# Two blocks of a weight tile begin 32 bytes further at the entries of the gate and up passes

## The chip, the cores and the metric

The kernel runs on one core of one Trainium2 chip. The metric is the device time of one execution in microseconds; of several runs the median is given. A profiled execution is a run of its own: its span reaches from the first to the last instruction, and its time is a little longer.

## The reference

The reference is a small decoder trunk in float32: 256 tokens of width 1024, two layers. Each layer has an attention (16 heads of 64; the first layer with forget gates, the second with a relative-position bias, both causal), a SwiGLU feed-forward part and a gated embedding, and a last RMSNorm ends the trunk. The change lies in the feed-forward part:

```python
u = _rmsnorm(h, ffn_norm_g[i])
gu = u @ ffn_w_in[i]                       # (256, 1024) @ (1024, 2 * 2816)
h = h + (jax.nn.silu(gu[..., :D_FF]) * gu[..., D_FF:]) @ ffn_w_out[i]
```

## The kernel before

All weights are packed into one array of 216 tiles, in the order in which they are used, each of 128 partitions x 1024 float32. `half` (line 110) brings in the next tile: SP starts its DMA into `raw` (six buffers), ScalarE rounds it to float32r as `hi` (line 122), and VectorE writes the remainder `raw - hi` as `lo` (line 123). `hi` and `lo` have six buffers each, in tiles of 1024 + 64 columns.

Every product of two float32 operands a and b is made of three matmuls in `mm3` (lines 76 to 80), all into the same accumulator: hi of a with hi of b (line 78), hi of a with lo of b (line 79), lo of a with hi of b (line 80). a is the operand that stays in the array, its weights; b streams through. So of three matmuls two load weights from the hi of a and the third from its lo.

There are two ways to use a tile of the packed array. In the q and k projections and in the gate and up passes the tile holds eight blocks of 128 columns, one for each 128 rows of the contraction, and a block is the weights; the normalised activations g (128 x 256 for each block) stream. `blocks` (line 126) makes these. In the other products (v, wo, the second feed-forward product fo, pu, pg) the weights are activations, and the tile streams in pieces of 512 columns, in the last gate partly of 256.

Where the operands lie: all tiles named here begin at a multiple of 256 bytes, which the kernel calls a line (`LINE = 64` float32). `blocks` asks `half` for a start 16 columns further (`APART = 16`), that is 64 bytes past the line; a block is 512 bytes long, so all its eight blocks begin 64 bytes past a line. g, and tiles that stream, begin on a line.

The feed-forward part (`ffn`) works in pieces f of 128 of the 2816 hidden columns, 22 in all. For each f there are two tiles, gate (a = 0) and up (a = 1), each of 8 blocks x 3 = 24 matmuls into bank gu. `up([0, 1])` is written apart, since the norm's second half is made in its midst. Behind it the order of TensorE's work is, in each layer:

- f = 2: the gate tile, then the four matmuls of `nm.spread` (pr, line 175), then the up tile
- f = 3: gate and up
- down for f = 0 and 1: 24 matmuls of 512 columns into the four banks fo
- f = 4, 5: gate, up, gate, up, without a break: 96 matmuls; then down for f = 2 and 3
- and so on to f = 20, 21, behind which the last down products, the embedding's product pu and the residual follow.

All work of an engine is issued in program order. A tile's DMA and its two passes on ScalarE and VectorE are issued as far ahead as the six buffers let them.

Names that the profile uses: gu is the accumulator of gate and up, whi and wlo are the hi and lo tiles, fh and fl the hi and lo of the gated product, pq the accumulator of the q and k projections, sp the attention scores, L78 to L80 the three matmuls of `mm3`.

Of the kernel before, what the change touches and what calls it, by code (L numbers as in the profile page):

```python
# [28 lines left out]
F32R = mybir.dt.float32r  # L29
AF = mybir.ActivationFunctionType  # L30
ALU = mybir.AluOpType

P = 128
S = 256
D = 1024
KT = D // P
# [10 lines left out]
HW = 1024  # L47
# [7 lines left out]
LINE = 64  # L55
APART = 16


@with_exitstack
def trunk(ctx: ExitStack, tc: tile.TileContext, x, xt, pt, w, wf, cst, gains, gf, bf, rel, hot, rvm, out):  # L60
    nc = tc.nc
    one = ctx.enter_context(tc.tile_pool(name="one", bufs=1))
    work = ctx.enter_context(tc.tile_pool(name="work", bufs=2))
# [4 lines left out]
    def bank(name):  # L68
        return ps.tile([P, 512], F32, tag="bank", name=name)

    def f32(ap):
        return ap.bitcast(F32)
# [3 lines left out]
    def mm3(o, a, b, start, stop):  # L76
        (ah, al), (bh, bl) = a, b
        mm(o, ah, bh, start=start, stop=False, skip_group_check=True)  # L78
        mm(o, ah, bl, start=False, stop=False, skip_group_check=True)  # L79
        mm(o, al, bh, start=False, stop=stop, skip_group_check=True)  # L80
# [26 lines left out]

    state = {"next": 0}

    def half(at=0):  # L110

        i = state["next"]
        state["next"] += 1
        raw = work.tile([P, HW], F32, tag="raw", bufs=RAW, name=f"raw{i}")
        hi, lo = (work.tile([P, HW + LINE], F32R, tag=n, bufs=6, name=f"{n}{i}")[:, at:at + HW] for n in ("whi", "wlo"))
        parts = 2 if i < 2 else 1
        for q in range(parts):
            c = slice(q * HW // parts, (q + 1) * HW // parts)
            if i == 0 and q == 1:
                nc.sync.dma_start(hx[:, 1], xt[:, 1])  # L120
            nc.sync.dma_start(raw[:, c], w[i][:, c])
            nc.scalar.activation(hi[:, c], raw[:, c], AF.Copy)  # L122
            nc.vector.tensor_tensor(lo[:, c], raw[:, c], f32(hi[:, c]), op=ALU.subtract)  # L123
        return hi, lo

    def blocks():

        return [t.rearrange("p (k c) -> p k c", k=KT) for t in half(APART)]


    class Norm:
# [51 lines left out]

    nm = Norm(0)
    first = [half()]
    nm.block(0, hx[:, 0])
    nm.block(1, hx[:, 1])
    first.append(half())
    for b in range(1, 4):
        nc.sync.dma_start(hx[:, 2 * b:2 * b + 2], xt[:, 2 * b:2 * b + 2])  # L190
# [29 lines left out]
    def split(hi, lo, src):  # L220
        nc.scalar.activation(hi, src, AF.Copy)  # L221
        nc.vector.tensor_tensor(lo, src, f32(hi), op=ALU.subtract)

    def tokens(o, x, t, w, start, stop):

        at = slice(t * P, (t + 1) * P)
        mm3(o, (x[0][:, at], x[1][:, at]), w, start, stop)
# [10 lines left out]
    def residual(hf, bks):  # L238
        for t in range(2):
            at = h[:, t, hf * HC:(hf + 1) * HC]  # L240
            nc.vector.tensor_tensor(at, at, bks[t], op=ALU.add)
# [67 lines left out]
    def attention(layer, nm, mid, early, nf):  # L309
        vb = [bank(f"v{layer}_{b}") for b in range(4)]  # L310
        rest = None
        for c in range(4):
            wt = [early.pop(0) if early else half() for _ in range(2)]
            for kk in range(2):
                hi, lo = wt[kk]
                k = 2 * c + kk
# [23 lines left out]
        for t in range(2):  # L340
            for hf in range(2):
                col = nm.col[:, t:t + 1]
                src = vb[2 * t + hf].rearrange("p (j s d) -> p j s d", s=2, d=DH)
                for s in range(2):
                    at = (slice(None), slice(4 * hf, 4 * hf + 4), slice(2 * s * DH, (2 * s + 1) * DH))
# [13 lines left out]
        def project(j, a):  # L359
            hi, lo = blocks()  # L360
            if a == 0:
                pq[j] = bank(f"pq{layer}_{j}")
            bk = pq[j]
            for k in range(KT):
                mm3(bk[:, a * S:(a + 1) * S], (hi[:, k], lo[:, k]), nm.k(k),
                    start=(k == 0), stop=(k == KT - 1))
            if a == 0:
                return
            del pq[j]
            t = work.tile([P, 2, S], F32, tag="qkt", name=f"qkt{layer}_{j}")  # L370
            nc.vector.tensor_tensor(t.rearrange("p a s -> p (a s)"), bk,
                                    nm.row.rearrange("p a s -> p (a s)"), op=ALU.mult)
            th = work.tile([P, 2, S], F32R, tag="qkh", name=f"qkh{layer}_{j}")
            tl = work.tile([P, 2, S], F32R, tag="qkl", name=f"qkl{layer}_{j}")
            split(th, tl, t)
            qk[j] = t, th, tl
# [54 lines left out]
        for j in range(NP):  # L431
            project(j, 0)
            if j >= 1:
                scores(j - 1)
            if j >= 2:
                transposes(j - 2)
            project(j, 1)
            if j >= 2:
                values(j - 2)
            if layer == 0 and j >= 4:  # L440
                moba[0](j - 4)
# [23 lines left out]
    def ffn(layer, nm, filler, np_):  # L465
        acc = []
        prod = {}

        def up(fs):

            bks = {f: bank(f"gu{layer}_{f}") for f in fs}

            def step(f, a, wt, k, start):
                mm3(bks[f][:, a * S:(a + 1) * S], (wt[0][:, k], wt[1][:, k]), nm.k(k), start, k == KT - 1)

            if fs[0] == 0:
                wts = {f: (blocks(), blocks()) for f in fs}
                for k in range(KT):
                    if k == 3:
                        nm.turn(1)  # L480
                        nm.square(1)
                    for f in fs:
                        for a in range(2):
                            step(f, a, wts[f][a], k, k == 0 and a == 0)
                nm.root()
                return fs, bks
            for a in range(2):
                wt = blocks()
                for k in range(KT):
                    step(fs[0], a, wt, k, k == 0)  # L490
                if fs[0] == 2 and a == 0:
                    nm.spread()
                    gated(*early)
            gated(fs, bks)

        def gated(fs, bks):
            for f in fs:
                t = work.tile([P, 2, S], F32, tag="t2k", bufs=3, name=f"gut{layer}_{f}")
                nc.vector.tensor_tensor(t.rearrange("p a s -> p (a s)"), bks[f],  # L499
                                        nm.row.rearrange("p a s -> p (a s)"), op=ALU.mult)  # L500
                sg = work.tile([P, S], F32, tag="sg", name=f"sg{layer}_{f}")
                nc.scalar.activation(sg, t[:, 0], AF.Silu)
                nc.vector.tensor_tensor(sg, sg, t[:, 1], op=ALU.mult)  # L503
                th = work.tile([P, S], F32R, tag="th", bufs=4, name=f"fh{layer}_{f}")
                tl = work.tile([P, S], F32R, tag="tl", bufs=4, name=f"fl{layer}_{f}")
                split(th, tl, sg)
                prod[f] = th, tl

        def down(f, wt):
            hi, lo = wt  # L510
            for t in range(2):
                for hf in range(2):
                    cols = slice(hf * HC, (hf + 1) * HC)
                    tokens(acc[hf][t], prod[f], t, (hi[:, cols], lo[:, cols]), f == 0, False)

        def last(f, hf):

            wt = half()
            for i in range(2):
                for t in range(2):  # L520
                    tokens(acc[hf][t], prod[f + i], t, [w[:, i * HC:(i + 1) * HC] for w in wt],
                           False, f + i == FT - 1)

        early = up([0, 1])
        acc.extend([bank(f"fo{layer}_{hf}_{t}") for t in range(2)] for hf in range(2))
        for f in range(2, FT, 2):
            up([f])
            up([f + 1])
            if f == FT - 6:
                pp = filler()  # L530
            if f < FT - 2:
                down(f - 2, half())
                down(f - 1, half())
        last(FT - 4, 0)
        filler(pp)
        last(FT - 2, 0)
        residual(0, acc[0])
        last(FT - 4, 1)
        np_.turn(0)
        np_.square(0)  # L540
        last(FT - 2, 1)
        residual(1, acc[1])
# [106 lines left out]
    for layer in range(2):  # L649
# [8 lines left out]
        nm = Norm(3) if layer == 0 else None  # L658
# [95 lines left out]
```

## Time and profile before

| what | value |
|---|---|
| time, median of 3 runs | 683.77 us (682.6 to 684.1) |
| the profiled execution's time | 684.86 us |
| its span | 683.1 us |
| TensorE busy with matmuls | 669.7 us, 98% of the span |
| TensorE loading weights | 614.9 us |
| VectorE busy | 453.3 us |
| ScalarE busy | 385.6 us |
| gu matmuls | 3 x 704 |

A matmul in a timeline has the start in microseconds, then how long it took. It is pipelined: the next one starts long before it is over, so what the stream costs is the distance from start to start, here called the pitch. The stretches that the profile can be asked for have the length, then for each engine the busy time with the count of instructions in brackets, and then the granted clock of TensorE (1.00 is full speed), the share of the DMA engines and the bytes moved in GB/s.

### The profile page before, as it was taken

To read this page: it belongs to the slowest core of one execution; us is meant where nothing else is said; L and a number is where in the kernel's file an instruction comes from. 1 tells how busy PE (TensorE), PEld (TensorE's weight loads), DVE (VectorE), ACT (ScalarE), POOL (GpSimd) and SP (SyncE) were. 2 spreads that over 40 slices of the span, in tenths; PEclk is the share of its full clock that TensorE was granted. 3 is DMA by queue.
4 is the path that set the end of the run, shared out by engine and by line. 5 is a ranking of instruction groups with operands and counts; after the bars stand their busy time and mean duration, and the time that the engine had idled before them with its cause. 6 is when DMAs were issued, how large, how long until landed. Compare 5 with 4: busy or idle time off the path is not lost.

```text
span 683.1 us, 11825 instructions
## 1 busy us (share of the span) xinstructions
PE 669.7 (98%) x4604; PEld 614.9 (90%) x4604; DVE 453.3 (66%) x782; ACT 385.6 (56%) x698; POOL 29.8 (4%) x57
## 2 busy tenths in 40 slices
PE   8998999999999999999999999999999999999994
PEld 6898998999999999998889999889999999999884
DVE  4688886666666666666676888765766666666673
ACT  6875665655444444447665766655544444444663
POOL 1057000000000000000000000000000000000000
PEclk9999999999999999999999999999999999999998
DMA  8979333455555555655576533343755555565401
GB/s 272 380 279 350 126 125 124 154 184 187 187 190 188 191 190 195 202 185 186 176 275 201 180 124 126 119 159 123 243 190 187 185 186 187 190 202 195 168 1 62
DMA packets 37529, 125.90 MB, mean 184 GB/s; under 512 B 4240, under 2 KB 7008, under 8 KB 37472
## 3 DMA queue, kind: packets, MB, share of 16 engines
q1 hardware_dynamic: 36016, 121.35, 52.5%
q0 software_dynamic: 608, 2.11, 1.0%
q10 hardware_dynamic: 848, 1.68, 0.7%
q8 instruction: 36, 0.59, 0.4%
q14 instruction: 21, 0.17, 0.1%
HBM read 124.03 MB, written 4.24 MB: 188 GB/s over the span
## 4 chain that ended last, share of the span: by engine, by line
PE 90%; DVE 0%; ACT 0%; issue 0%; POOLq 0%; DVEq 0%; POOL 0%; ACTq 0%
PE gu L80 12%; PE gu L79 12%; PE gu L78 12%; PE fo L78 6%; PE fo L79 6%; PE fo L80 6%; PE pq L78 4%; PE pq L80 4%; PE pq L79 4%; PE wo L78 2%; PE wo L80 2%; PE wo L79 2%; PE pg L78 2%; PE pg L80 2%; PE pg L79 2%; PE pp L413 2%
## 5 line engine op out<-in xcount | busy, mean ns | idle before, releaser
L123 DVE TENSOR_TENSOR wlo<-raw,whi 128x1024 fp32r<-128x1024 f32 (+1 forms) x218 | 264.9, 1218 | 162.6 <-ACT whi L122 162.4
L122 ACT ACTIVATE whi<-raw 128x1024 fp32r<-128x1024 f32 (+1 forms) x218 | 227.7, 1048 | 196.0 <-PE gu L79 75.0
L78 PE MATMUL gu<-g,whi 128*128 128x256 f32 x704 | 198.5, 282 | 0.0
L80 PE MATMUL gu<-g,wlo 128*128 128x256 f32 x704 | 198.2, 282 | 0.0
L79 PE MATMUL gu<-g,whi 128*128 128x256 f32 x704 | 198.1, 281 | 0.0
L79 PEld LDWEIGHTS gu<-g,whi 128*128 128x128 f32 x704 | 134.8, 191 | 0.7
L78 PEld LDWEIGHTS gu<-g,whi 128*128 128x128 f32 x704 | 132.4, 188 | 0.8
L80 PEld LDWEIGHTS gu<-g,wlo 128*128 128x128 f32 x704 | 132.4, 188 | 0.0
L78 PE MATMUL pq<-g,whi 128*128 128x256 f32 x256 | 74.7, 292 | 0.0
L80 PE MATMUL pq<-g,wlo 128*128 128x256 f32 x256 | 72.4, 283 | 0.0
L79 PE MATMUL pq<-g,whi 128*128 128x256 f32 x256 | 72.3, 283 | 0.0
L78 PE MATMUL fo<-whi,fh 128*128 128x512 f32 x176 | 69.0, 392 | 0.0
L79 PE MATMUL fo<-wlo,fh 128*128 128x512 f32 x176 | 68.8, 391 | 0.0
L80 PE MATMUL fo<-whi,fl 128*128 128x512 f32 x176 | 68.5, 389 | 0.0
L78 PEld LDWEIGHTS pq<-g,whi 128*128 128x128 f32 x256 | 48.9, 191 | 0.9 <-ACT vhi L347 0.6
L79 PEld LDWEIGHTS pq<-g,whi 128*128 128x128 f32 x256 | 49.3, 193 | 0.0
L80 PEld LDWEIGHTS pq<-g,wlo 128*128 128x128 f32 x256 | 49.0, 191 | 0.0
L221 ACT ACTIVATE fh<-sg 128x256 fp32r<-128x256 f32 x44 | 18.1, 415 | 47.6 <-DVE sg L503 47.6
L499 DVE TENSOR_TENSOR gut<-gu,row 128x512 f32<-128x512 f32 x44 | 30.0, 691 | 18.0 <-PE gu L80 18.0
L80 PEld LDWEIGHTS fo<-whi,fl 128*128 128x128 f32 x176 | 33.1, 188 | 7.0
L78 PEld LDWEIGHTS fo<-whi,fh 128*128 128x128 f32 x176 | 33.0, 188 | 6.3
L79 PEld LDWEIGHTS fo<-wlo,fh 128*128 128x128 f32 x176 | 33.1, 188 | 6.0
(137 smaller groups left out, 935.5 us busy)
## 6 DMA issues: line engine op xcount, KB each, us to landing
raw<-w SPq DMA_DIRECT2D x214, 512.0 KB, 3.3
d<-d SPq DMA_DIRECT2D x4, 768.0 KB, 12.5
bias<-cd POOLq DMA_DIRECT2D x4, 512.0 KB, 9.2
bias<-d SPq DMA_DIRECT2D x4, 512.0 KB, 5.1
raw<-w SPq DMA_DIRECT2D x4, 256.0 KB, 5.4
h<-x ACTq DMA_DIRECT2D x2, 512.0 KB, 5.3
hx<-xt SPq DMA_DIRECT2D x3, 256.0 KB, 5.3
p<-pt SPq DMA_DIRECT2D x2, 256.0 KB, 4.2
```

The source lines that it names most:

```text
L78: mm(o, ah, bh, start=start, stop=False, skip_group_check=True)
L79: mm(o, ah, bl, start=False, stop=False, skip_group_check=True)
L80: mm(o, al, bh, start=False, stop=stop, skip_group_check=True)
L122: nc.scalar.activation(hi[:, c], raw[:, c], AF.Copy)
L123: nc.vector.tensor_tensor(lo[:, c], raw[:, c], f32(hi[:, c]), op=ALU.subtract)
L221: nc.scalar.activation(hi, src, AF.Copy)
L413: nc.tensor.transpose(pp[:, q * P:(q + 1) * P], e[:, q * P:(q + 1) * P], ident)
L499: nc.vector.tensor_tensor(t.rearrange("p a s -> p (a s)"), bks[f], nm.row.rearrange("p a s -> p (a s)"), op=ALU.mult)
```

## The change

In some tiles the first two blocks of lo begin 32 bytes further than the others: `FURTHER = 8` columns are added to the 16 of `APART`, so they begin 96 bytes past the line. The other six begin one line behind their former place, so again 64 bytes past a line. `hi` stays as it was. To make room the lo tiles are one line wider, all of them. VectorE writes such a lo in two instructions, one for the two first blocks and one for the six others, where it wrote one.

These tiles are, in each layer, the up tile of f = 2 and the gate tile of each even f from 4 on: the tile with which a stretch of gate and up matmuls begins anew behind other work of TensorE. The tiles of `up([0, 1])` and those of the q and k projections aren't among them. The rest of the diff hands the blocks on as lists in place of one rearranged view.

```diff
+ENTRY = 2
+FURTHER = 8
...
-        hi, lo = (work.tile([P, HW + LINE], F32R, tag=n, bufs=6, name=f"{n}{i}")[:, at:at + HW] for n in ("whi", "wlo"))
+        hi = work.tile([P, HW + LINE], F32R, tag="whi", bufs=6, name=f"whi{i}")[:, at:at + HW]
+        lt = work.tile([P, HW + 2 * LINE], F32R, tag="wlo", bufs=6, name=f"wlo{i}")
+        lo = lt[:, at:at + HW]
+        if entry:
+            nc.sync.dma_start(raw, w[i])
+            nc.scalar.activation(hi, raw, AF.Copy)
+            ats = [(at + FURTHER, 0, entry), (at + LINE, entry, HW)]
+            for a, c0, c1 in ats:
+                nc.vector.tensor_tensor(lt[:, a + c0:a + c1], raw[:, c0:c1], f32(hi[:, c0:c1]), op=ALU.subtract)
+            return hi, [lt[:, a + k * P:a + (k + 1) * P] for a, c0, c1 in ats for k in range(c0 // P, c1 // P)]
...
-    def blocks():
-
-        return [t.rearrange("p (k c) -> p k c", k=KT) for t in half(APART)]
+    def blocks(entry=False):
+
+        hi, lo = half(APART, ENTRY * P if entry else 0)
+        hi = [hi[:, k * P:(k + 1) * P] for k in range(KT)]
+        return hi, lo if entry else [lo[:, k * P:(k + 1) * P] for k in range(KT)]
...
             for a in range(2):
-                wt = blocks()
+                wt = blocks(a == 1 if fs[0] == 2 else a == 0 and fs[0] % 2 == 0)
```

More of the change, by code (lines that the diff above doesn't have):

```diff
@@ L108, in trunk, with half @@
     state = {"next": 0}
-    def half(at=0):
+    def half(at=0, entry=0):
         i = state["next"]
@@ L364, in project @@
             for k in range(KT):
-                mm3(bk[:, a * S:(a + 1) * S], (hi[:, k], lo[:, k]), nm.k(k),
+                mm3(bk[:, a * S:(a + 1) * S], (hi[k], lo[k]), nm.k(k),
                     start=(k == 0), stop=(k == KT - 1))
@@ L473, in step @@
             def step(f, a, wt, k, start):
-                mm3(bks[f][:, a * S:(a + 1) * S], (wt[0][:, k], wt[1][:, k]), nm.k(k), start, k == KT - 1)
+                mm3(bks[f][:, a * S:(a + 1) * S], (wt[0][k], wt[1][k]), nm.k(k), start, k == KT - 1)
             if fs[0] == 0:
```

## The prediction

> **What bounds the kernel now.** I read the page from the top, then what TensorE waits for, then the distance from the start of one matmul to the start of the next.
>
> ```profile
> span 683.1 us, 11825 instructions
> ...
> PE 669.7 (98%) x4604; PEld 614.9 (90%) x4604; DVE 453.3 (66%) x782; ACT 385.6 (56%) x698; POOL 29.8 (4%) x57
> ...
> PE 90%; DVE 0%; ACT 0%; issue 0%; POOLq 0%; DVEq 0%; POOL 0%; ACTq 0%
> PE gu L80 12%; PE gu L79 12%; PE gu L78 12%; PE fo L78 6%; PE fo L79 6%; PE fo L80 6%; PE pq L78 4%; PE pq L80 4%; PE pq L79 4%; PE wo L78 2%; PE wo L80 2%; PE wo L79 2%; PE pg L78 2%; PE pg L80 2%; PE pg L79 2%; PE pp L413 2%
> ```
>
> The chain that ends last is TensorE, and the largest part of it is gu, the gate and up passes (3 x 12%). The view of waits for TensorE shows that it hardly waits; its three longest:
>
> ```profile
> PE sp L386 <- DVE qkl L222: 1.8, 1, 1.8
> PE pg L78 <- ACT pgt L571: 1.4, 1, 1.4
> PE v L78 <- ACT g L142: 1.3, 1, 1.3
> ```
>
> 4.5 us, none of it in gu. So the time of gu is its count of matmuls times their pitch (start to start), and no engine's wait can be won there. Is the pitch a floor? The view of stretches, restricted to tile gu, gives two stretches of four tiles each, one of each layer (columns: stretch, its length, PE busy with the count, and so on, the granted clock behind them):
>
> ```profile
> 158.88:170.18 11.30, 11.30 (x96) 11.26 (x95) 0.69 (x1) 1.00 0.58 189
> 487.60:498.91 11.31, 11.31 (x96) 11.26 (x95) 0.69 (x1) 1.00 0.59 188
> ```
>
> 11.305/96 = 117.8 ns at a granted clock of 1.00, alike in both layers. Now the same form (128x128 weights 64 bytes past the line, 256 columns of g on the line) in the q and k projection of layer 1, from the timeline, its second to fourth and its last matmul of 72:
>
> ```profile
> 368.44 0.29 PE L79 MATMUL pq<-g,whi 128*128 128x256 f32 x1
> 368.57 0.28 PE L80 MATMUL pq<-g,wlo 128*128 128x256 f32 x1
> 368.68 0.28 PE L78 MATMUL pq<-g,whi 128*128 128x256 f32 x1
> ...
> 376.39 0.28 PE L80 MATMUL pq<-g,wlo 128*128 128x256 f32 x1
> ```
>
> From the fourth to the 72nd: 7.71 us over 68 pitches = 113.4 ns. Same instruction, same offsets, 4.4 ns less, and it holds through three tiles of weights. The next pass of the same projection, entered behind the score matmuls, is at the gu pitch again:
>
> ```profile
> 377.83 0.28 PE L78 MATMUL pq<-g,whi 128*128 128x256 f32 x1
> ...
> 383.01 0.28 PE L80 MATMUL pq<-g,wlo 128*128 128x256 f32 x1
> ```
>
> From its fourth matmul to the last of 48, 5.18 us over 44 pitches: 117.7 ns. So this stream has **two steady pitches**, and it is the entry that chooses. How little decides is seen where gu begins after the same pr matmuls that stood ahead of the pq at 113.4:
>
> ```profile
> 145.05 0.28 PE L79 MATMUL gu<-g,whi 128*128 128x256 f32 x1
> 145.17 0.28 PE L80 MATMUL gu<-g,wlo 128*128 128x256 f32 x1
> 145.29 0.28 PE L78 MATMUL gu<-g,whi 128*128 128x256 f32 x1
> ...
> 153.41 0.39 PE L78 MATMUL fo<-whi,fh 128*128 128x512 f32 x1
> ```
>
> These are the second to fourth of 72, and the fo behind them. The second pitch is 0.12 us where that pq had 0.13; after that one hold-up of about 0.01 us it ran at 113.4 for 7.7 us, while this one stays at (153.41 - 145.29)/69 = 117.7 ns. A third one stands in the last layer's gate, where the operands lie otherwise: weights from g and columns from whi and wlo, all on the line.
>
> ```profile
> 667.94 0.28 PE L78 MATMUL pg<-whi,g 128*128 128x256 f32 x1
> ...
> 670.10 0.28 PE L78 MATMUL pg<-whi,g 128*128 128x256 f32 x1
> ```
>
> 18 pitches in 2.16 us: 120.0 ns. So the pitch depends on where the operands lie and on how the stream was entered, and gu sits in the middle one of three.
>
> **The change part by part.** It touches twenty tiles of weights: in each layer the second of f = 2 and the first of f = 4, 6, ..., 20. Behind each the next tiles are entered with no break, so a pitch chosen there governs 72 matmuls (f = 2, the up tile, and both of f = 3) or 96 (two f, two tiles each, 24 matmuls a tile): 2 x (72 + 9 x 96) = 1872 of the 2112 in gu.
>
> *The moved operands.* In such a tile the third matmul (lo of block 0) and the sixth (lo of block 1) read weights 96 bytes past the line in place of 64; the other 22 read as before (256 + 64 is 64 past the next line). The chip shows no operand at 96, so I bound the cost of one such matmul. Below: nothing, it takes 117.8 ns or 113.4. Above: the largest irregular pitch of a running stream near it, the 0.13 us of 368.44 to 368.57, some 12 ns more; twenty tiles with two of them make 40 x 12 = 0.5 us. I take 0.25 us, half of that, since a hold-up of that kind is what preceded the pitch of 113.4. By itself this is nothing; the question is the pitch it leaves behind.
>
> *The gain, if the pitch changes.* All 1872 matmuls at 113.4 in place of 117.8 is 1872 x 4.4 ns = 8.2 us. The first six of each entry are still counted at the old pitch: 20 x 6 x 4.4 = 0.5 us. Less the 0.25 us of hold-ups: 8.2 - 0.5 - 0.25 = **7.5 us**. From both sides: 0 if the pitch doesn't change; 8.2 plus the irregular start of the fo stretches behind it if all goes well. For these:
>
> ```profile
> 170.18:175.65 5.47, 5.47 (x24) 4.33 (x24) 0.00 (x0) 1.00 0.58 192
> ```
>
> that is 227.9 ns a matmul, and a quiet stretch of this form is at 226.7:
>
> ```profile
> 664.18 0.39 PE L78 MATMUL pg<-whi,g 128*128 128x512 f32 x1
> ...
> 666.90 0.39 PE L78 MATMUL pg<-whi,g 128*128 128x512 f32 x1
> ```
>
> 12 pitches in 2.72 us; so 24 x 1.2 ns = 0.03 us at each of twenty, 0.6 us; I count none of it.
>
> *VectorE.* In these tiles one subtraction of 1024 columns becomes two, of 256 and of 768. From the groups by shape:
>
> ```profile
> L123 DVE TENSOR_TENSOR wlo<-raw,whi 128x1024 fp32r<-128x1024 f32 x214 | 262.2, 1228 | 155.6 <-ACT whi L122 155.4
> L503 DVE TENSOR_TENSOR sg<-sg,gut 128x256 f32<-128x256 f32 x44 | 18.3, 419 | 0.0
> L123 DVE TENSOR_TENSOR wlo<-raw,whi 128x512 fp32r<-128x512 f32 x4 | 2.7, 690 | 6.9 <-ACT whi L122 6.9
> ```
>
> 256 columns: 419 ns; 768: halfway between 690 and 1228, 959 ns; together 1378, or 150 ns more, 3.0 us in twenty, on an engine that is busy 66% of the span. What hides it is the lead of the tile over its use. The first of f = 4 is the 43rd tile of weights (8 for v, 16 for pq, 8 for wo, 8 for f = 0 to 3, 2 for fo are ahead of it), so the 45th L123 writes it, since the first two tiles have two each; and 45 have begun by 147.9:
>
> ```profile
> 0.00:147.90 147.90, 53.20 (x45) 0.99 0.62 217
> ...
> 146.66 1.22 DVE L123 TENSOR_TENSOR wlo<-raw,whi 128x1024 fp32r<-128x1024 f32 x1
> ...
> 159.11 0.28 PE L80 MATMUL gu<-g,wlo 128*128 128x256 f32 x1
> ```
>
> Done at 147.88, first read at 159.11: 11.2 us of lead against 0.15 us. The raw buffer is released 0.15 us later, so SP's next load of a tile starts that much later, with the same lead over it. Without the cover it would be 0.15 us an entry, 3 us. The two writes are two marks for TensorE to wait on; both are long past. Cost: nothing.
>
> *The tile.* lo grows by one line of 256 bytes, so the six buffers still begin on a line, and what lies behind them moves by whole lines. The gu stretches above agree within 0.01 us over buffers that lie at different lines, so I cost this at nothing.
>
> Sum, against the profiled execution: span 683.1 - 7.5 = 675.6; that execution took 684.86 with 1.76 us around the span. The median of the runs is 683.77, so I forecast 683.77 - 7.5 = **676.3 us**.
>
> **The rivals.** A difference of less than 0.2%, 1.4 us here, is about what a measurement of this kernel can't tell from no change.
>
> *Nothing lasts.* The two moved blocks shift the stream, and it falls back to 117.8 within a few matmuls. For it: all the gu stretches shown, entered behind fo and behind pr, are at this pitch, so it attracts strongly. Against: the pq at 113.4 shows that a hold-up of 12 ns is enough, and that the pitch then holds. Time: 683.77 with 0.25 us of hold-ups, 684.0.
> The Trainium skill, SBUF — State Buffer, "Who interferes with whom", gives TensorE separate read ports for weights and moving columns and says that "PE and ACT never wait on anyone"; by that rule the place of a weight block would change no time, and the result would be this rival. The trace does not bear it out for these streams: one form has 113.4, 117.8 and 120.0 ns at a granted clock of 1.00.
>
> *A longer pitch.* The displaced blocks put the reads of weights and columns in step in the way of the pg stretch, and the 1872 matmuls run at 120.0: 1872 x 2.2 = 4.1 us, 687.9 us. It decides from 0.7 ns a matmul on (1.4 us/1872), a pitch of 118.5. For it: that pitch exists for this form of instruction. Against: it is seen only with all operands on the line, and in none of the stretches of gu or pq above, with weights at 64, and 22 of 24 matmuls of the tile still read at 64.
>
> *Half of it.* The pitch of 113.4 is reached behind fo but lost at one of the changes of tile or in one layer: half, 8.2/2 - 0.5 = 3.6 us, 680.2 us. Against it: the three tiles of pq at 113.4 without a break, and twenty entries that look alike.
>
> **How the numbers follow.** Forecast 0.48, half of it 0.12, nothing lasts 0.20, a longer pitch 0.20. Faster by over 0.2%: 0.60; within: 0.20; slower: 0.20. The range leaves out the longer pitch: from 674.8 (8.2 plus 0.6 us of the fo starts, 675.0, and the spread of the runs) to 684.6 (nothing lasts, with both hold-ups at 12 ns, and the spread).
>
> **What would show it.** Right: the gu stretches of 96 take 10.9 us (96 x 113.4) and not 11.3, from the first to the last of the twenty, with the pitch changing within the first six matmuls; the wait view of TensorE names nothing new; L123 appears with 256 and 768 columns and no later lo. Wrong: a stretch that still takes 11.30 (nothing lasts), or 11.52 (120 ns). The prediction is also wrong if fo or pq changes its pitch, which I hold fixed, or if TensorE begins to wait on L123.

## The result and the profile after

| | median | runs |
|---|---|---|
| before | 683.42 us | 4, from 682.6 to 684.1 |
| after | 675.67 us | 4, from 675.14 to 677.16 |
| after / before | 0.9898 | 95% interval 0.9884 to 0.9911 |

The change takes 1.0% off: 7.75 us between the medians; by the ratio, which is not that of these two medians, 7.0 us, and 6.1 to 7.9 by its interval. The forecast was 676.3 us.

The page of the kernel after, its span and its busy engines. The three matmul lines of `mm3` are L82 to L84 now, the two instructions of an ordinary tile L136 and L137, those of a displaced one L125 and L128.

```profile
span 674.2 us, 11845 instructions
PE 658.9 (98%) x4604; PEld 604.1 (90%) x4604; DVE 455.1 (67%) x802; ACT 386.1 (57%) x698; POOL 31.5 (5%) x57
```

As many matmuls as before, 10.8 us less of them (3.8 us of it ahead of the first gu, where TensorE is busy 121.7 us and was busy 125.5), and VectorE busy 1.8 us longer with twenty instructions more. TensorE's three longest waits are the same three as before, and none stands in gu:

```profile
PE sp L402 <- DVE qkl L238: 2.2, 2, 1.3
PE pg L82 <- ACT pgt L587: 1.4, 1, 1.4
PE v L82 <- ACT g L158: 1.2, 1, 1.2
```

The stretches of gu in the kernel after (length, PE with its count, loads, VectorE, granted clock, DMA share, GB/s): the first and the last of the eighteen stretches of 96 that are entered behind fo, and then a stretch of 72 that is entered behind pr.

```profile
157.07:167.99 10.92, 10.92 (x96) 10.88 (x95) 0.69 (x1) 1.00 0.62 200
613.31:624.22 10.91, 10.91 (x96) 10.87 (x95) 0.69 (x1) 1.00 0.56 193
143.04:151.61 8.57, 8.57 (x72) 8.52 (x72) 1.88 (x3) 1.00 0.91 294
```

All eighteen lie at 10.914 us, from 11.307: 0.393 us each, 18 x 0.393 = 7.07 us. The two of 72, one in each layer, take what they took before (8.56). How the pitch changes is seen at an entry, in the timeline of the kernel after:

```profile
157.07 0.28 PE L82 MATMUL gu<-g,whi 128*128 128x256 f32 x1
157.19 0.28 PE L83 MATMUL gu<-g,whi 128*128 128x256 f32 x1
157.31 0.28 PE L84 MATMUL gu<-g,wlo 128*128 128x256 f32 x1
157.44 0.28 PE L82 MATMUL gu<-g,whi 128*128 128x256 f32 x1
157.56 0.28 PE L83 MATMUL gu<-g,whi 128*128 128x256 f32 x1
157.67 0.28 PE L84 MATMUL gu<-g,wlo 128*128 128x256 f32 x1
```

The trace's own starts, in ns, give the pitches 118, 120, 124, 122, 117 and then 113, 113, 114 to the end of the stretch. The first displaced block is the L84 at 157.31: one hold-up of 12 ns in all is spread about it (those five pitches make 601 ns, five of 117.8 make 589), and from the sixth matmul on the stream is at 113.4. The second displaced block, the L84 at 157.67, comes when that is over.

Does this hold the whole difference? Two stages, before and then after, in the view of stretches with all engines (behind the loads stand VectorE, ScalarE and GpSimd): from layer 0's first gu to layer 1's first v, and the projections and attention of layer 1, which the change doesn't touch.

```profile
129.48:345.19 215.71, 215.71 (x1477) 200.33 (x1476) 138.19 (x176) 112.74 (x165) 1.41 (x2) 1.00 0.57 187
368.24:431.41 63.17, 63.17 (x559) 61.13 (x558) 51.57 (x151) 45.00 (x116) 0.00 (x0) 1.00 0.43 143
```

```profile
127.67:339.85 212.18, 212.18 (x1478) 196.76 (x1476) 138.90 (x186) 113.20 (x165) 1.41 (x2) 1.00 0.58 190
362.89:426.07 63.18, 63.18 (x560) 61.13 (x558) 51.57 (x151) 45.01 (x117) 0.00 (x0) 1.00 0.44 142
```

Layer 0's feed-forward stage gives 3.53 us, which is 9 x 0.393; layer 1's gives 3.54. The projections give nothing. The spans of the two profiles differ by 8.9 us, so 1.8 us lie ahead of the first gu, at 129.48 us before and 127.67 after. Those aren't the change's: in before one stretch of pq fell to a granted clock of 0.66, in after the same stretch did not.

```profile
54.76:58.95 4.19, 4.19 (x24) 4.15 (x24) 0.00 (x0) 0.66 1.02 385
```

```profile
54.24:57.15 2.91, 2.91 (x24) 2.86 (x24) 0.00 (x0) 1.00 1.01 375
```

That is 1.28 us of it; another 1.41 is the first stretch of v (14.38 and 12.97 us), and other stretches take some back. One stretch of pq changed its pitch as well: the 48 matmuls behind sp in layer 0 took 5.852 us in before (117.8 ns) and 5.640 in after (113.4 ns). They stand ahead of every displaced block, and the experiments whose work up to there is that of after have both: 113.4 in e1, e2, e6 and e7, 117.8 in e3 and e5. So the instructions don't always settle the pitch of an entry: up to there these programs are the same. In six experiments that leave everything ahead of gu alone (e1, e2, e3, e5, e6, e7) the first gu starts between 126.9 and 129.2 us. The medians, with 7.75, hold the same scatter.

### The profile page after: what moved, and what is told of

Its sections match the earlier page's. It is cut to its first block, busy times and chain, and to the rows that moved or that the text cites. A ratio compares the mean times of both kernels' runs of the same rounds, so it can differ in the third digit from the quotient of the medians.

```text
span 674.2 us, 11845 instructions
## 1 busy us (share of the span) xinstructions
PE 658.9 (98%) x4604; PEld 604.1 (90%) x4604; DVE 455.1 (67%) x802; ACT 386.1 (57%) x698; POOL 31.5 (5%) x57
## 4 chain that ended last, share of the span: by engine, by line
PE 91%; DMA 3%; ACT 2%; DVE 2%; issue 1%; SPq 0%; POOLq 0%; ACTq 0%; DVEq 0%; POOL 0%
PE gu L84 12%; PE gu L82 12%; PE gu L83 12%; PE fo L82 6%; PE fo L83 6%; PE fo L84 6%; PE pq L82 4%; PE pq L84 4%; PE pq L83 4%; PE wo L82 2%; PE wo L84 2%; PE wo L83 2%; PE pg L82 2%; PE pg L84 2%; PE pg L83 2%; DMA raw<-w 2%
## 5 line engine op out<-in xcount | busy, mean ns | idle before, releaser
L137 DVE TENSOR_TENSOR wlo<-raw,whi 128x1024 fp32r<-128x1024 f32 (+1 forms) x198 | 240.8, 1219 | 137.7 <-ACT whi L136 137.5
L136 ACT ACTIVATE whi<-raw 128x1024 fp32r<-128x1024 f32 (+1 forms) x198 | 206.7, 1049 | 159.1 <-PE gu L83 48.2
L82 PE MATMUL gu<-g,whi 128*128 128x256 f32 x704 | 195.5, 278 | 0.0
L84 PE MATMUL gu<-g,wlo 128*128 128x256 f32 x704 | 195.1, 277 | 0.0
L83 PE MATMUL gu<-g,whi 128*128 128x256 f32 x704 | 195.1, 277 | 0.0
L82 PEld LDWEIGHTS gu<-g,whi 128*128 128x128 f32 x704 | 132.6, 188 | 0.8
L84 PEld LDWEIGHTS gu<-g,wlo 128*128 128x128 f32 x704 | 132.1, 188 | 0.0
L82 PE MATMUL pq<-g,whi 128*128 128x256 f32 x256 | 73.8, 288 | 0.0
L84 PE MATMUL pq<-g,wlo 128*128 128x256 f32 x256 | 71.7, 280 | 0.0
L83 PE MATMUL pq<-g,whi 128*128 128x256 f32 x256 | 71.6, 280 | 0.0
L82 PE MATMUL fo<-whi,fh 128*128 128x512 f32 x176 | 68.9, 391 | 0.0
L84 PE MATMUL fo<-whi,fl 128*128 128x512 f32 x176 | 68.5, 389 | 0.0
L82 PEld LDWEIGHTS pq<-g,whi 128*128 128x128 f32 x256 | 48.1, 188 | 0.9 <-issue 0.6
L83 PEld LDWEIGHTS pq<-g,whi 128*128 128x128 f32 x256 | 48.6, 190 | 0.0
L84 PEld LDWEIGHTS pq<-g,wlo 128*128 128x128 f32 x256 | 48.4, 189 | 0.0
L128 DVE TENSOR_TENSOR wlo<-raw,whi 128x256 fp32r<-128x256 f32 (+1 forms) x40 | 26.0, 688 | 22.5 <-ACT whi L125 22.5
L84 PEld LDWEIGHTS fo<-whi,fl 128*128 128x128 f32 x176 | 33.0, 188 | 7.0
L82 PEld LDWEIGHTS fo<-whi,fh 128*128 128x128 f32 x176 | 33.0, 188 | 6.2
```

What stands on the lines that cost most here:

```text
L128: nc.vector.tensor_tensor(lt[:, a + c0:a + c1], raw[:, c0:c1], f32(hi[:, c0:c1]), op=ALU.subtract)
```

## The experiments

The theory: a stream of these matmuls has several steady pitches; which one it runs at is settled at its entry and lasts; and a block of weights that lies 32 bytes off pushes a running stream from 117.8 to 113.4 ns. The rivals: the gain is of the widened lo tile or of its two writes; 96 bytes is a better place as such; the push needs two blocks, or the entry.

**e1: the same code, no displacement.**

```diff
-FURTHER = 8
+FURTHER = 0
```

> The changed kernel with the further 8 columns set to 0: the lo tiles are as wide, lo of an entry tile is written in two pieces and with the same distance of a line between them, but all eight blocks begin 64 bytes past a line. Theory (the displaced read pushes the running stream from the pitch of 117.8 ns to that of 113.4, which then lasts by itself): the 18 stretches of 96 take 11.31 us again, time 683.4 us. Rival (the wider tiles, what moves behind them or the two writes did it, and the place of the two blocks nothing): 10.91 us a stretch, 675.7 us.

Median of ten runs 682.58 us, before 682.54; ratio 1.0008, 95% interval 0.9993 to 1.0023. A stretch of gu in e1:

```profile
156.45:167.76 11.31, 11.31 (x96) 11.26 (x95) 0.69 (x1) 1.00 0.59 195
```

Wider tiles, a second write and the lists of blocks do nothing. The place of the displaced blocks does all of it.

**e2: one displaced block, not two.**

```diff
-ENTRY = 2
+ENTRY = 1
```

> Only block 0 of lo lies 96 bytes past the line, blocks 1 to 7 at 64. Theory in the form that one push is enough: in the changed kernel the pitches from the third matmul on were 124, 122, 117 and then 113 ns, before the sixth matmul, which is the second displaced one, can have done anything; so 10.91 us a stretch, 675.7 us. Rival (each displaced block does its share, two are needed): the stretch falls back to 117.8 ns, 11.3 us, 683 us.

One run, 677.51 us.

```profile
158.61:169.52 10.91, 10.91 (x96) 10.88 (x95) 0.69 (x1) 1.00 0.58 194
```

10.914 us again, in all eighteen. One block is enough; the second one neither helps nor costs.

**e3: the displaced tile is the second of the pair**, so that the push comes 24 matmuls behind the entry.

```diff
-                wt = blocks(a == 1 if fs[0] == 2 else a == 0 and fs[0] % 2 == 0)
+                wt = blocks(a == 1 and fs[0] % 2 == 0)
```

> The displaced blocks stand in the up tile (the second of four) of f = 2, 4, ..., 20 and no longer in the gate tile, so the push comes after 24 matmuls of a stretch that runs at 117.8 ns, not at its entry behind fo. Theory (any displaced read in a running stream pushes it): 24 matmuls at 117.8 and 72 at 113.4 with 13 ns for the push, 11.00 us a stretch, 677.3 us. Rival (it is the entry behind fo that the two blocks mend, and only there): 11.31 us a stretch, 683.4 us.

One run, 678.8 us. The first 24 matmuls of a stretch and the whole of it:

```profile
157.98:160.80 2.82, 2.82 (x24) 2.82 (x24) 0.00 (x0) 1.00 0.58 192
157.98:169.00 11.02, 11.02 (x96) 10.98 (x95) 0.69 (x1) 1.00 0.57 193
```

By the starts, 117.8 ns up to the displaced tile, then 118, 121, 124, 121, 117, 113. It isn't the entry: a running stream changes too, in the same five steps.

**e4: all blocks at 96**, hi and lo, on the kernel before.

```diff
-        return [t.rearrange("p (k c) -> p k c", k=KT) for t in half(APART)]
+        return [t.rearrange("p (k c) -> p k c", k=KT) for t in half(24)]
```

> The kernel before, with all weight blocks of the q, k, gate and up tiles, hi and lo, 96 bytes past the line in place of 64, one write a tile. Theory (the place sets which pitches can last, the displacement only gives the push): no push happens inside a stretch, since all blocks lie alike, so a stretch stays at one pitch from its entry on; of that pitch the theory says only that it is one of those seen, 113.4, 117.8 or 120.0 ns, so 10.9, 11.3 or 11.5 us a stretch. Rival (96 bytes is the better place, and the two blocks helped because they lay there): 113.4 ns in all streams of this form, q and k as well, from the first matmul on, 10.88 us a stretch and 3 to 4 us less in the projections, about 671 us.

One run, 682.77 us. A stretch of gu behind fo, and one of 72 behind pr, here with all engines and with the few matmuls of others at their edges:

```profile
156.94:168.20 11.26, 11.26 (x97) 11.26 (x96) 6.49 (x8) 4.85 (x6) 0.00 (x0) 1.00 0.55 188
471.68:480.40 8.72, 8.72 (x75) 8.72 (x74) 8.22 (x13) 5.68 (x9) 0.00 (x0) 1.00 0.96 325
```

11.264/96 = 117.3 ns, in uneven pitches from 115 to 120, and 8.724/72 = 121.2 ns, which is 120.0 once it runs. So 96 is no better place, and with all blocks alike there is no push: it takes a block that lies otherwise than its neighbours. The 117.3 is a value that the theory's list of pitches did not have.

**e5: the two blocks at 128 bytes, not 96.**

```diff
-FURTHER = 8
+FURTHER = 16
```

> The changed kernel with the two blocks 128 bytes past the line (further by 16 columns, 64 bytes) in place of 96. Theory in the form that any displacement by some ten columns pushes: 10.91 us in the 18 stretches of 96. Rival (it must be half of 64 bytes; a whole step of 64 leaves the reads in the same order): 11.31 us a stretch, 683 us.

One run, 676.27 us.

```profile
157.32:168.25 10.93, 10.93 (x96) 10.89 (x95) 0.69 (x1) 1.00 0.62 204
143.58:151.86 8.28, 8.28 (x72) 8.24 (x72) 1.87 (x3) 1.00 0.89 302
```

10.927, with the change only behind the second displaced block (118 119 118 122 119 117 122 119 113): 128 pushes too. Not foreseen was that the stretches of 72 change with it, in both layers, from 8.567 to 8.282.

**e6: a second push, given to a stream that is at 113.4 already**: both tiles of an even f are displaced.

```diff
-                wt = blocks(a == 1 if fs[0] == 2 else a == 0 and fs[0] % 2 == 0)
+                wt = blocks(a == 1 if fs[0] == 2 else fs[0] % 2 == 0)
```

> The changed kernel with two displaced blocks in the gate tile and in the up tile of each even f from 4 on, so that the second push meets a stream that already runs at 113.4 ns. Theory (the lower pitch holds against a displaced read, as it held against the sixth matmul's in the changed kernel): 10.91 to 10.93 us a stretch. Rival (a push changes the pitch whichever it is): 24 matmuls at 113.4 and 72 at 117.8, 11.2 us a stretch, 681 us.

One run, 677.42 us.

```profile
157.64:168.59 10.95, 10.95 (x96) 10.91 (x95) 0.69 (x1) 1.00 0.61 201
```

10.947, 0.033 us more than with one push and a little above what was expected; the rival's 11.2 did not come. But the pitch does not hold through the push, it comes back. The third and the sixth matmul of the up tile are the displaced ones; with them the matmul ahead of the third, and the one at which it is over:

```profile
160.50 0.28 PE L83 MATMUL gu<-g,whi 128*128 128x256 f32 x1
160.62 0.28 PE L84 MATMUL gu<-g,wlo 128*128 128x256 f32 x1
...
160.98 0.29 PE L84 MATMUL gu<-g,wlo 128*128 128x256 f32 x1
...
161.22 0.28 PE L83 MATMUL gu<-g,whi 128*128 128x256 f32 x1
```

Six pitches in 0.72 us, in ns 118, 117, 118, 119, 123, 119, between pitches of 113 on both sides. The first displaced block takes the stream to 117.8, and it is on its way back where the second stands. Whether the second brings it back or it comes back alone, e6 can't tell, since both blocks are in it; a tile with one displaced block, met by a stream at 113.4, was not run (e8 below has a sign of it).

**Why the 72 behind pr didn't change.** A sign of it stands among the weight loads. Grouped by shape over one stretch (count, busy us, mean ns of one), a stretch of 96 before:

```profile
L79 PEld LDWEIGHTS gu<-g,whi 128*128 128x128 f32 x32 | 6.1, 192 | 0.0
L80 PEld LDWEIGHTS gu<-g,wlo 128*128 128x128 f32 x32 | 6.0, 188 | 0.0
L78 PEld LDWEIGHTS gu<-g,whi 128*128 128x128 f32 x31 | 5.8, 188 | 0.0
```

At 117.8 ns the matmuls go in threes: one load of three takes 192 ns, the others 188. Behind fo the long one is the second, L79. In the stretch behind pr, the long one before and then after:

```profile
L80 PEld LDWEIGHTS gu<-g,wlo 128*128 128x128 f32 x24 | 4.6, 192 | 0.0
```

```profile
L82 PEld LDWEIGHTS gu<-g,whi 128*128 128x128 f32 x24 | 4.6, 192 | 0.0
```

Before it is the third, the lo itself; after, the first: the push did act there, it moved the long load on by one and left the pitch. In the stretches at 113.4 no load is long:

```profile
L83 PEld LDWEIGHTS gu<-g,whi 128*128 128x128 f32 x30 | 5.6, 188 | 0.0
```

Hence a rule of three, for blocks at 96: a displaced load right behind the long one brings 113.4; one that is the long one itself moves it on; one right ahead of the long one does nothing. At 128 (e5) it doesn't fit: there the first displaced load behind fo stands right behind the long one too, and the pitch changes only behind the second. The order of the three matmuls puts it to the test, since only lo is displaced.

**e7: lo first in the displaced blocks of f = 2**, so that behind pr the displaced load comes right behind the long third place.

```diff
+    def mm3_lo_first(o, a, b, start, stop):
+        (ah, al), (bh, bl) = a, b
+        mm(o, al, bh, start=start, stop=False, skip_group_check=True)
+        mm(o, ah, bh, start=False, stop=False, skip_group_check=True)
+        mm(o, ah, bl, start=False, stop=stop, skip_group_check=True)
...
-                mm3(bks[f][:, a * S:(a + 1) * S], (wt[0][k], wt[1][k]), nm.k(k), start, k == KT - 1)
+                fn = mm3_lo_first if f == 2 and a == 1 and k < ENTRY else mm3
+                fn(bks[f][:, a * S:(a + 1) * S], (wt[0][k], wt[1][k]), nm.k(k), start, k == KT - 1)
```

> The changed kernel; in the up tile of f = 2 alone, the two displaced blocks have their three matmuls in another order: lo of a first, then the two with hi of a. The stretch of 72 behind pr did not change its pitch in the changed kernel (8.57 us). In streams at 117.8 ns one weight load of three takes 192 ns and the others 188; behind fo, where the push worked, it is that of the second matmul (line 79), so the displaced third comes right behind it; behind pr in the kernel before it is that of the third itself. Theory (the push works when the displaced load comes right behind the long one): with lo first the fourth matmul of this stretch is displaced right behind a long third, and the 72 matmuls take 8.28 us, in both layers. Rival (a stream entered behind pr can't be pushed): 8.57 us.

One run, 674.61 us. The stretches of 72 of layer 0 and layer 1:

```profile
142.23:150.51 8.28, 8.28 (x72) 8.24 (x72) 1.87 (x3) 1.00 0.91 300
467.12:475.40 8.28, 8.28 (x72) 8.25 (x72) 1.88 (x3) 1.00 0.94 305
```

As the rule says. Lo first without a displacement was not run behind pr; within a stretch this order with the displaced blocks changes nothing (e10, next).

**e10 and e11: the rule within a stretch.** As e3, with lo first (e10: right ahead of the long second place) or lo second (e11: the long one itself); the third place, right behind the long one, is e3. The difference to e3, for e10 (`mm3_lo_first` is that of e7):

```diff
...
+                fn = mm3_lo_first if f >= 2 and f % 2 == 0 and a == 1 and k < ENTRY else mm3
...
```

> As the run with the displaced blocks in the up tile of every even f (25th matmul of a stretch of 96 on, which took 11.02 us with lo third), but in the two displaced blocks lo comes first of the three. In these stretches the long load of 192 ns is that of the second matmul. Theory (only a displaced load right behind the long one brings the stream to 113.4 ns): the displaced load now comes right ahead of the long one, nothing changes, 11.31 us a stretch; in the 72 behind pr, where the long one is the third, 8.28 us. Rival (any displaced load pushes, and behind pr it was another matter): 11.02 us a stretch.

> The same with lo second of the three, so that the displaced load is the long one itself. Theory: the stretch of 96 keeps its pitch, 11.31 us, and the long load moves on to the next of the three matmuls, as it did in the 72 behind pr in the changed kernel (from the third, line 84, to the first, line 82); there 8.56 us. Rival (any displaced load pushes): 11.02 us.

One run each, 681.56 and 681.64 us. A stretch of 96 and one of 72, first of e10 and then of e11:

```profile
155.69:167.00 11.31, 11.31 (x96) 11.26 (x95) 0.69 (x1) 1.00 0.57 192
141.91:150.19 8.28, 8.28 (x72) 8.24 (x72) 1.88 (x3) 1.00 0.92 326
```

```profile
155.92:167.23 11.31, 11.31 (x96) 11.27 (x95) 0.69 (x1) 1.00 0.59 195
142.16:150.42 8.26, 8.26 (x72) 8.22 (x72) 1.88 (x3) 1.00 0.96 329
```

The same 32 bytes in the same tile gain 0.29 us a stretch in the third place (e3) and nothing in the first or second. In e11 the long load goes one on, as the rule says; its loads ahead of the displaced tile and then behind it:

```profile
L83 PEld LDWEIGHTS gu<-g,whi 128*128 128x128 f32 x8 | 1.5, 192 | 0.0
```

```profile
L84 PEld LDWEIGHTS gu<-g,wlo 128*128 128x128 f32 x21 | 4.0, 192 | 0.0
```

The miss is e11's stretch of 72: 8.56 expected, 8.262 measured (pitches 202 120 117 116 114 113). Within a running stream the rule held in all three places (e3, e10, e11); directly at an entry it isn't complete.

**e8 and e12: more entries displaced**, on the kernel after: the k tiles of the projections and the first gate tile.

```diff
-            hi, lo = blocks()
+            hi, lo = blocks(j >= 2 and a == 1)
...
-                wts = {f: (blocks(), blocks()) for f in fs}
+                wts = {f: (blocks(f == 0), blocks()) for f in fs}
```

> The changed kernel with displaced blocks also in the second tile of each projection pair behind the transposes pp (j from 2 on, twelve stretches of 24 matmuls of pq, in the kernel before with the long load on the second matmul, line 79) and in the first tile of f = 0. Theory: each of the twelve goes from 2.91 to 2.84 us, less 0.02 for the push; about 0.9 us in all, and the first 36 matmuls of gu from 4.25 to 4.15 us in both layers; 674.6 us. Rival (short stretches behind other work don't take the push, as the one behind pr didn't): 2.91 us each, 675.7 us.

> The kernel with displaced blocks also behind pp and in the tile of f = 0, again, timed in several rounds; its one run before took 673.28 us. From the stretches of that profile it should lie 0.4 us a layer below the changed kernel in the feed-forward parts and 1.4 us below it in the projections of layer 1, and about as much in those of layer 0 if their wait for the bias does not take it back: 673 to 674 us, 0.985 to 0.987 of the kernel before. Rival (a stretch that is shorter is given back at the next wait of the attention, as in the run with still more displaced blocks): 675 to 676 us, 0.989.

One run 673.28 us; timed as e12, 673.63 us (672.36 to 674.49, 5 runs) to 682.61 before, ratio 0.9864, 95% interval 0.9844 to 0.9884. This is the fastest version here; the change has 0.9898, and the two intervals just touch, at 0.9884. A pq stretch behind pp before, and in e8 one behind pp and one behind po:

```profile
72.85:75.76 2.91, 2.91 (x24) 2.86 (x24) 0.00 (x0) 1.00 0.34 89
```

```profile
71.27:74.11 2.84, 2.84 (x24) 2.80 (x24) 0.00 (x0) 1.00 0.38 98
75.15:78.06 2.91, 2.91 (x24) 2.78 (x24) 0.00 (x0) 1.00 0.11 20
```

2.910 to 2.837 where a tile is displaced, and the undisplaced one behind po comes from 3.003 to 2.909 with it, which was not foreseen. Eleven of the twelve did so, in e8 as in e12; one, in layer 0, kept 2.91. The projections and attention of layer 1, in e12:

```profile
361.12:422.88 61.76, 61.76 (x560) 59.89 (x558) 51.80 (x157) 45.00 (x116) 0.00 (x0) 1.00 0.46 146
```

1.41 us less than the 63.17 before. Not all of it comes from the displaced tiles and the stretches right behind them. The 48 matmuls behind sp, which have no displaced block, take 5.658 us where they took 5.853: 0.19 us. And the order of TensorE's matmuls, the same in before, in after and in e1 to e7, e10 and e11, is another here: before, a q tile of layer 1 was cut by the po matmuls into 2, 1 and 21, and in e8 and e12 it is whole; that block of po and pq takes 3.95 us where it took 4.23: 0.28 us less, where the blocks that were whole before lose 0.12.

The stretches of 72 lie at 8.282 here as well, without lo first. Their pitches are 206 116 114 113 118 117 118 122 118 114 113 (e8, layer 0): the stream enters at the low pitch, leaves it about the second displaced block (the sixth matmul), and comes back with no displaced block behind that one. In the stretch ahead of them the long load stood on another of the three lines than in after; whether that decides the entry was not settled.

**e9: more still**, e8 with lo first in e7's tile and in the q tiles from the fourth on, behind po.

```diff
-            hi, lo = blocks()
+            push = j >= 2 if a else j >= 3
+            hi, lo = blocks(push)
...
+                fn = mm3_lo_first if push and a == 0 and k < ENTRY else mm3
```

> The changed kernel with displaced blocks at more entries: the tile of the first f (f = 0), the second tile of each projection pair from j = 2 on (behind pp, lo third as everywhere), the first tile of each pair from j = 3 on (behind po, where the long load stands on the third matmul, so with lo first in the two displaced blocks), and the up tile of f = 2 with lo first. Theory: besides the 18 stretches of 96 at 10.91 us, the twelve of pq behind pp take 2.84 us, the ten behind po 2.93 in place of 3.00, the first 36 of gu 4.15 in place of 4.25, the 72 behind pr 8.28 in place of 8.56; against the changed kernel about 0.9 + 0.7 + 0.2 + 0.6 = 2.4 us less, 673.3 us, 0.985 of the kernel before. Rival (the order of the three has nothing to do with it): the stretches behind po stay at 3.00 us, 674 us.

676.4 us (675.03 to 677.69, 5 runs) to 682.5 before, ratio 0.9903, 95% interval 0.9885 to 0.9922: a miss. Layer 1's projections and attention take 63.11 us, 1.35 more than in e12. In e9 TensorE's order is another once more, though the edit names no order between tiles: it differs from that of before at 28 of 4604 matmuls (e8 and e12 at 4). In the timeline three matmuls of a q tile stand ahead of the last two po.

```profile
392.17 0.39 PE L452 MATMUL po<-tf,vf 128*128 128x128 f32 x2
392.32 0.37 PE L88 MATMUL pq<-g,wlo 128*128 128x256 f32 x1
392.52 0.28 PE L89 MATMUL pq<-g,whi 128*128 128x256 f32 x1
392.64 0.28 PE L90 MATMUL pq<-g,whi 128*128 128x256 f32 x1
392.76 0.38 PE L452 MATMUL po<-tf,vf 128*128 128x128 f32 x2
```

A block of ten po and 24 pq, cut so in e9 and whole in e12:

```profile
391.28:395.54 4.26, 4.26 (x36) 4.00 (x34) 3.69 (x10) 2.13 (x5) 0.00 (x0) 1.00 0.41 147
```

```profile
388.38:392.33 3.95, 3.95 (x37) 3.82 (x35) 3.70 (x10) 2.30 (x8) 0.00 (x0) 1.00 0.25 88
```

0.31 us a cut. Layer 1 has two, and one block of scores and pp in pieces (1.90 us where e12 has 1.40); with two pq stretches that kept 2.91 (0.15) and three behind po at 2.935 where e12's undisplaced ones have 2.908 (0.08), that is 0.62 + 0.50 + 0.15 + 0.08 = 1.35 us, all of the difference. The five stretches behind po that stayed whole are at 2.935, as expected and not at the rival's 3.00. Two of them, behind a stretch that kept 2.91, enter at the higher pitch and are pushed; the other three enter at the lower one, as in e12, and only lose by the displaced blocks. Why the order came out otherwise was not tried.

## Why the prediction was right, and where not

**What bounds gu.** Right: the count of matmuls times the pitch. In gu the time went down by the pitch alone, with the waits as they were.

**Two pitches, chosen and then kept.** Right, and shown: e1 against after leaves the place of the blocks as the only difference, 11.307 against 10.914 us. The Trainium skill's rule that "PE and ACT never wait on anyone" (SBUF — State Buffer, "Who interferes with whom"), by which the place of a weight block changes no time, is not borne out for these streams in the sense that the prediction read it: those two numbers differ by 3.5% at a granted clock of 1.00. Whom the stream waits for, another engine or TensorE's own reads, no run here shows. Of the entry the prediction said too much: e3 shows that a stream can be pushed in its midst, and the 48 pq matmuls show that the same entry can come out either way.

**The sum.** 7.5 us forecast, 7.07 measured in the stretches. By the forecast's own terms a stretch of 96 gives 96 x 4.4 ns less six matmuls at the old pitch (26 ns) and the hold-ups (12 ns): 0.384 us, and 0.393 was measured. The eighteen were to give 6.9 us and gave 7.07.

**The step that failed** is "All 1872 matmuls": 144 of them, the two stretches of 72 behind pr, stayed at 117.8. The forecast gave them 2 x (72 x 4.4 - 38) = 0.56 us and they gave none. The "twenty entries that look alike" don't: the long load of three stood elsewhere behind pr, which the rows of before already held and the prediction didn't read. For these two, "nothing lasts" came true; for the eighteen it didn't.

**The hold-ups.** One of 12 ns at each entry, not two; the second block costs nothing (e2); it meets a stream that is still changing.

**The rest.** The fo stretches stayed at 5.466 us, so the 0.6 us that were left out were rightly left out. The two subtractions, grouped by shape in the kernel after:

```profile
L128 DVE TENSOR_TENSOR wlo<-raw,whi 128x768 fp32r<-128x768 f32 x20 | 19.0, 951 | 0.0
L128 DVE TENSOR_TENSOR wlo<-raw,whi 128x256 fp32r<-128x256 f32 x20 | 8.5, 424 | 22.5 <-ACT whi L125 22.5
```

951 and 424 ns where 959 and 419 were taken, and no wait of TensorE in gu: the lead covered them. A change of pitch in pq was named as a sign of being wrong, and one stretch of pq did change (5.852 to 5.640 us); it stands ahead of the first displaced block and takes either value in programs that are the same up to there, so it is no effect of the displacement.

**A longer pitch** of 120.0 did not come with the displaced blocks. It came in e4, behind pr, with all weights at 96; the reason given against it, that most weights still read at 64, fits that.

That the time fell by 7.75 us between the medians, nearer to 7.5 than the stretches' 7.07, is scatter ahead of gu and no merit of the sum.

## What to carry to other kernels

Where an engine is busy without a wait, compare the start-to-start distance of its longest stream with that of the same instruction elsewhere in the trace: a difference of 4% at a full clock is time that no wait shows. Try the place of an operand before reordering work, give it a control that changes everything but the place (e1 here), and count the gain only over the entries at which the stream really is the same, down to the duration of its weight loads. Look at the same stretch in more than one run, since a pitch can differ between two of them. Read the order of the instructions again after any edit: in e9 a reordering that nobody asked for cost what the edit was to gain, and in e12 one gave a part of the gain.

## What the runs showed of the hardware that was not expected

- The same float32r matmul of 256 columns with 128x128 weights has at least four steady rates at a clock of 1.00: 113.4, 117.3 (e4), 117.8 and 120.0 ns.
- A stream at 117.8 ns has one weight load of 192 ns in three and two of 188; at 113.4 all take 188, but so do they at 117.3 (e4). In a running stream a displaced load counts by its place to the long one (e3, e10, e11, blocks at 96).
- A stream at 113.4 ns that meets two more displaced blocks is at 117 to 123 ns for six matmuls, 33 ns in all, and then at 113.4 again (e6).
- Behind the same instructions a stream ran at 113.4 ns in some runs (after, e1, e2, e6, e7) and at 117.8 in others (e3, e5): the 48 pq matmuls behind sp in layer 0.
- What in the chip makes the cycle of three is open. The runs show what moves it, not what it is.
